# Strassen's seven products for pairs of up-projection tiles in a float32 two-layer trunk

## The chip, the cores and the metric

The kernel runs on one core of a Trainium2 chip. The metric is the time of one execution on the device in microseconds (us); three timed runs of the kernel before took 1123.32, 1124.51 and 1124.87.

## What is computed

512 tokens of 1024 features pass four sub-layers in float32: gated linear attention, an MLP, sliding-window attention, an MLP. Each is wrapped in norms, x <- x + RMSNorm_post(f(RMSNorm_pre(x))). The change concerns the MLPs, with D_FF = 4096:

```python
def sq_relu_mlp(h, w_up, w_down):
    return jnp.square(jax.nn.relu(h @ w_up)) @ w_down

for i in range(DEPTH):                      # DEPTH = 2
    h = rms_norm(x, ln_mix_pre[i])
    ...                                     # m: the token mixer of this layer
    x = x + rms_norm(m, ln_mix_post[i])
    h = rms_norm(x, ln_mlp_pre[i])
    f = sq_relu_mlp(h, mlp_w_up[i], mlp_w_down[i])
    x = x + rms_norm(f, ln_mlp_post[i])
```

## The kernel before

**Precision.** TensorE multiplies in a reduced float32 form. Every operand is split in two: h, a copy in that form by ScalarE (L83), and l, the rest, a subtraction by VectorE (L84, two inputs in SBUF). A product is three matmuls, h by h (L150), h by l (L151) and l by h (L152), `mm3`.

**Up projection.** `prenorm` scales each of four token tiles (128 tokens), transposes it on TensorE (L190) and splits it into four pairs of tiles hT, which hold features by tokens. The hidden features are made transposed: 32 tiles of 128 hidden features by 512 tokens, one accumulator each, eight k tiles of 128 features, three matmuls of 512 columns per k tile (`t_tile`, `t_step`). A tile's weights are one DMA of 512 KB into a `rawp` buffer (`weight`), split in halves of 512 columns. The first four tiles (NAHEAD) run earlier, in `t_ahead`: the matmuls of the first 256 tokens while the last token tiles of the sub-layer before are still being finished, then those of the other 256. ScalarE takes the Relu from PSUM (L702) and VectorE squares (L703).

**Down projection.** `natural` does two halves of 512 output features. For each of 32 k tiles `lhs` splits the hidden tile into two buffers (h, l) of the pool `tp` (17 buffers of 512 columns, `half`), and twelve matmuls follow: four token tiles by three. In the second half the last eight k tiles (TAIL) run token tile by token tile, and behind each one `evac`, `finish` and the next sub-layer's `prenorm` run: GpSimd computes the inverse roots in chains of five small operations (L124, L125, L127, L131, L132), ahead of which L182 or L216 prepares a term.

**Order.** Each engine executes its own queue in order. The order is set when the program is built, by a scheduler that follows priorities and dependencies; `later` and `tick` tie some instructions of the tail to matmuls. Buffers come from pools: `sp` (25 buffers of 1024 columns, `slot`), `tp` 17, `wp` 10 for split weights, `rawp` 3, and four PSUM pools of two banks (mm, ob, sc, tp). An instruction that writes into a buffer waits for the last reader of what was there. GpSimd has no work in the up stage.

Of the kernel before, what the change touches and what calls it, by code (L numbers as in the profile page):

```python
# [14 lines left out]
P = 128  # L15
# [13 lines left out]
ROWS = (slice(0, 64), slice(64, 128))  # L29
# The first steps in their order, each with its token tile or weight and half of the columns:  # L30
# P idle products, X load tokens, B spread the norm's gain, C load the identity, W load weights, q mean square,
# x gain, r root, s scale, t transpose, h and w split.
START = "P1 X0a P3 X0b X1 B0 C0 W0 W1 W2 q0 q1 x0a r0 s0a x0b X2 x1a t0a w0a x1b X3 s0b w1a s1a h0a t0b w0b t1a w2a w1b q2 W3 x2a s1b t1b h1a h0b x2b s2a h1b w2b t2a h2a w3a s2b q3 t2b w3b x3a h2b s3a x3b s3b t3a t3b h3a h3b"
# [5 lines left out]
def trunk(ctx: ExitStack, tc: tile.TileContext, x, vecs, g_qk, g_vg, g_lr, g_up, g_norm, g_out,  # L39
# [4 lines left out]
    const = ctx.enter_context(tc.tile_pool(name="const", bufs=1))  # L44
    rawp = ctx.enter_context(tc.tile_pool(name="rawp", bufs=3))
    wp = ctx.enter_context(tc.tile_pool(name="wp", bufs=10))
# [3 lines left out]
    tp = ctx.enter_context(tc.tile_pool(name="tp", bufs=17))  # L50
    st = ctx.enter_context(tc.tile_pool(name="st", bufs=64))
    ppool = {n: ctx.enter_context(tc.tile_pool(name="p" + n, bufs=b, space=bass.MemoryType.PSUM))
# [101 lines left out]
    def behind(insts, target):  # L154
        """Issue order only: the instructions come after the target on their engine."""
        for i in insts:
            tc.add_manual_dep(i.ins, target.ins.name, NOSYNC, reason="order")
# [3 lines left out]
    def later(when, insts):  # L161
        """Keeps instructions behind the matmul that ends this piece of a sub-layer's last part."""
        if ticks[0] is not None:
            plan.setdefault(when, []).extend(insts)
# [6 lines left out]
    def new_hT():  # L171
        return [(slot([P, 2, T], F32R, "hTh"), slot([P, 2, T], F32R, "hTl")) for _ in range(NK // 2)]

    def prenorm(t, wpre, hT):
# [10 lines left out]
        for q in range(2):  # L185
            part = slice(q * 512, (q + 1) * 512)
            later(4 * t + SCALE, [act.activation(xw[:, part], xw[:, part], AF.Copy, scale=r)])
            tb = tbank([P, 4, P])
            for k in range(4):
                later(4 * t + TURN, [pe.transpose(tb[:, k, :], xw[:, q * 512 + k * P:q * 512 + (k + 1) * P], ident)])  # L190
            for kk in range(2):
                h, l = hT[2 * q + kk]
                split(h[:, :, cols], l[:, :, cols], tb[:, 2 * kk:2 * kk + 2, :])
# [78 lines left out]

    def t_step(acc, w, hT, k, cols):
        (wh, wl), (h, l) = w, hT[k // 2]
        mm3(acc[:, cols], wh[:, k * P:(k + 1) * P], wl[:, k * P:(k + 1) * P],
            h[:, k % 2, cols], l[:, k % 2, cols], k == 0, k == NK - 1)

    def t_steps(src, hT, evac, n=None):
        """One T tile in pieces."""
        w = weight(src)  # L280
        acc = bank(n=n)
        for k in range(NK):
            t_step(acc, w, hT, k, slice(0, T))
            if k % 2 and k < NK - 1:
                yield
        evac(acc)
        yield

    def outer_steps(lhs, wd, acc):
        """The products for one half of the columns in pieces, all tokens at each k tile."""  # L290
        for kp in range(NK // 2):
# [39 lines left out]

# [1 line left out]
    def gla(hT, first, post, done):  # L333
# [229 lines left out]

# [1 line left out]
    def swa(hT, post, done):  # L565
# [35 lines left out]
        def queries():  # L601
            """The query heads' products in pieces."""
            for j in range(2, 8):
# [89 lines left out]

# [1 line left out]
    def mlp(layer, hT, post, done):  # L695
        a = []

        def ev(i, acc):
            if i % 2 == 0:
                a.append(slot([P, 2, T]))  # L700
            aa = a[-1][:, i % 2, :]
            act.activation(aa, acc, AF.Relu)  # L702
            dve.tensor_mul(aa, aa, aa)  # L703

        accs = t_ahead([m_up[layer, i] for i in range(NAHEAD)], hT)
        for i in range(NAHEAD):
            ev(i, accs[i])
        for i in range(NAHEAD, NF):
            ev(i, t_tile(m_up[layer, i], hT))

        def lhs(n, kp):
            r = []
            for i in range(2):
# [3 lines left out]
                else:  # L717
                    h, l = half([P, T], F32R), half([P, T], F32R)
                split(h, l, a[kp][:, i, :])
                r.append((h, l))  # L720
            return r
        natural(lhs, m_down[layer], NF, post.evac, TAIL, done)

# [1 line left out]
    warm = half([P, 512], F32R)  # L725
# [8 lines left out]
    def put(i):  # L734
        """Keeps the start's instructions on their engine in the order of START."""
        e = i.ins.engine
# [74 lines left out]
    for layer in range(2):  # L811
        nxt = new_hT()
        wpost, wpre = bcast(vecs[layer, 1]), bcast(vecs[layer, 2])
# [90 lines left out]
```

## Time and profile before

| | |
|---|---|
| timed runs, median | 1124.51 us (1123.32 to 1124.87) |
| profiled execution, span | 1120.4 us |
| TensorE (PE) busy | 1095.0 us, 98% |
| VectorE (DVE) busy | 592.0 us, 53% |
| ScalarE (ACT) busy | 523.3 us, 47% |
| GpSimd (POOL) busy | 107.7 us, 10% |
| moved by DMA | 108.11 MB, mean 96 GB/s |

The span is the time from the first to the last instruction of one profiled execution; the profile gives no other time for it, so the runs' median stands beside it. Busy is the time in which at least one instruction of the engine was under way; TensorE's weight loads have a row of their own (PEld) and overlap its matmuls. In the rows, "x<-a,b 128x512" is an operation with output x and inputs a and b, by the program's names. "[1.27 <-ACT xw L187]" behind a row is idle time ahead of it and what ended it. The first number of a timeline row is its start, the second its length; matmuls overlap, so their cost is read from start to start.

### The profile page before, as it was taken

To read this page: it belongs to the slowest core of one execution; us is meant where nothing else is said; L and a number is where in the kernel's file an instruction comes from. 1 tells how busy PE (TensorE), PEld (TensorE's weight loads), DVE (VectorE), ACT (ScalarE), POOL (GpSimd) and SP (SyncE) were. 2 spreads that over 40 slices of the span, in tenths; PEclk is the share of its full clock that TensorE was granted. 3 is DMA by queue.
4 is the path that set the end of the run, shared out by engine and by line. 5 is a ranking of instruction groups with operands and counts; after the bars stand their busy time and mean duration, and the time that the engine had idled before them with its cause. 6 is when DMAs were issued, how large, how long until landed. Compare 5 with 4: busy or idle time off the path is not lost.

```text
span 1120.4 us, 14561 instructions
## 1 busy us (share of the span) xinstructions
PE 1095.0 (98%) x5372; PEld 913.2 (82%) x5372; DVE 592.0 (53%) x1135; ACT 523.3 (47%) x1142; POOL 107.7 (10%) x283
## 2 busy tenths in 40 slices
PE   8999999999999999999999999999999999999997
PEld 5778887889888888888888899879888888888886
DVE  5676538476333334447427889667433334447423
ACT  6764435465323334446326688556432223446420
POOL 1021112250000000000015000043000000000002
PEclk9999999999999999999999999999999999999999
DMA  7412222223332223222223532104322232222212
GB/s 251 134 65 84 76 77 73 76 82 127 99 105 98 94 94 94 94 94 94 94 76 133 168 97 76 54 22 136 110 95 95 100 105 96 94 94 94 94 38 76
DMA packets 32153, 108.11 MB, mean 96 GB/s; under 512 B 3921, under 2 KB 4177, under 8 KB 32082
## 3 DMA queue, kind: packets, MB, share of 16 engines
q1 hardware_dynamic: 32082, 107.19, 29.4%
q8 instruction: 42, 0.69, 0.3%
q14 instruction: 29, 0.24, 0.1%
HBM read 100.88 MB, written 2.10 MB: 92 GB/s over the span
## 4 chain that ended last, share of the span: by engine, by line
PE 82%; POOL 5%; DVE 5%; ACT 3%; issue 2%; DMA 2%; SPq 0%; DVEq 0%; POOLq 0%; ACTq 0%
PE mm L150 15%; PE mm L152 15%; PE mm L151 15%; PE ob L151 5%; PE ob L152 5%; PE ob L150 5%; PE sc L152 3%; PE sc L151 3%; PE sc L150 3%; POOL st L125 2%; ACT junk L180 1%; POOL st L127 1%; PE sb L625 1%; POOL st L124 1%; PE pT L654 1%
## 5 line engine op out<-in xcount | busy, mean ns | idle before, releaser
L83 ACT CAST wh<-raw 128x512 fp32r<-128x512 f32 x348 | 206.5, 618 | 359.3 <-PE mm L151 236.7
L84 DVE TENSOR_TENSOR wl<-raw,wh 128x512 fp32r<-128x512 f32 x348 | 232.4, 691 | 253.3 <-ACT wh L83 253.1
L150 PE MATMUL mm<-hTh,wh 128*128 128x512 f32 x448 | 174.3, 389 | 0.0
L151 PE MATMUL mm<-hTl,wh 128*128 128x512 f32 x448 | 174.3, 389 | 0.0
L152 PE MATMUL mm<-hTh,wl 128*128 128x512 f32 x448 | 174.3, 389 | 0.0
L84 DVE TENSOR_TENSOR t<-s,t 128x512 fp32r<-128x512 f32 x112 | 77.5, 692 | 126.6 <-PE ob L151 66.8
L83 ACT CAST t<-s 128x512 fp32r<-128x512 f32 x112 | 69.4, 619 | 65.5 <-PE ob L152 42.8
L152 PEld LDWEIGHTS mm<-hTh,wl 128*128 128x128 f32 x448 | 84.1, 188 | 17.6
L151 PEld LDWEIGHTS mm<-hTl,wh 128*128 128x128 f32 x448 | 84.1, 188 | 17.4
L150 PEld LDWEIGHTS mm<-hTh,wh 128*128 128x128 f32 x448 | 84.1, 188 | 17.2
L151 PE MATMUL mm<-wl,t 128*128 128x512 f32 x224 | 88.3, 394 | 0.0
L150 PE MATMUL mm<-wh,t 128*128 128x512 f32 x224 | 88.2, 394 | 0.0
L152 PE MATMUL mm<-wh,t 128*128 128x512 f32 x224 | 88.2, 394 | 0.0
L216 POOL TENSOR_SCALAR st<-st 128x1 f32<-128x1 f32 x16 | 4.4, 277 | 554.0 <-ACT junk L212 520.7
L150 PEld LDWEIGHTS mm<-wh,t 128*128 128x128 f32 x224 | 42.0, 188 | 10.4 <-ACT s L702 0.5
L151 PE MATMUL ob<-wl,t 128*128 128x512 f32 x128 | 50.5, 394 | 0.0
L152 PE MATMUL ob<-wh,t 128*128 128x512 f32 x128 | 50.4, 393 | 0.0
L150 PE MATMUL ob<-wh,t 128*128 128x512 f32 x128 | 50.4, 393 | 0.0
L151 PEld LDWEIGHTS mm<-wl,t 128*128 128x128 f32 x224 | 42.1, 188 | 9.8
L152 PEld LDWEIGHTS mm<-wh,t 128*128 128x128 f32 x224 | 42.1, 188 | 9.7
L703 DVE TENSOR_TENSOR s<-s 128x512 f32<-128x512 f32 x64 | 43.8, 685 | 0.0
L151 PE MATMUL sc<-wl,t 128*128 128x512 f32 x96 | 37.9, 394 | 0.0
(292 smaller groups left out, 2249.9 us busy)
## 6 DMA issues: line engine op xcount, KB each, us to landing
raw<-in_m_up_dram SPq DMA_DIRECT2D x64, 512.0 KB, 3.4
raw<-in_m_down_dram SPq DMA_DIRECT2D x64, 512.0 KB, 3.4
raw<-in_g_vg_dram SPq DMA_DIRECT2D x16, 512.0 KB, 3.5
raw<-in_s_qkv_dram SPq DMA_DIRECT2D x10, 512.0 KB, 4.1
raw<-in_g_qk_dram SPq DMA_DIRECT2D x8, 512.0 KB, 4.4
raw<-in_g_out_dram SPq DMA_DIRECT2D x8, 512.0 KB, 3.6
q<-hl SPq DMA_DIRECT2D x32, 128.0 KB, 2.5
raw<-in_s_out_dram SPq DMA_DIRECT2D x8, 512.0 KB, 3.8
```

Of the source, the lines that this page charges most:

```text
L83: act.copy(h, src)
L84: dve.tensor_sub(l, src, f(h))
L124: pool.tensor_scalar(v, ss, scale, base, ALU.mult, ALU.add)
L125: pool.tensor_tensor(r0, v, mhalf[:, :n], ALU.pow)
L127: pool.tensor_scalar(t, v, r0, r0, ALU.mult, ALU.mult)
L150: pe.matmul(out_ap, lhsT=lh, rhs=rh, start=first, stop=False)
L151: pe.matmul(out_ap, lhsT=lh, rhs=rl, start=False, stop=False)
L152: newest[0] = pe.matmul(out_ap, lhsT=ll, rhs=rh, start=False, stop=last)
L180: act.activation(junk, xt[:, part], AF.Square, accum_out=ss[:, i:i + 1])
L625: newest[0] = pe.matmul(sb[:, e, :], lhsT=q[:, e, pc], rhs=k2[:, i, win], start=i == 0, stop=i == 1)
L654: pe.transpose(tb[:, e, jj, :], p[:, e, c:c + P], ident)
L703: dve.tensor_mul(aa, aa, aa)
```

## The change

For each MLP the 32 up tiles are seen as two rows of 16 (tile i and tile i+16), the 1024 input features as two halves (512 each, q = 0, 1), the tokens as two halves of 256. So a pair of tiles is a 2x2 block product: 2 blocks of hidden features, 2 of tokens, summed over 2 of input features. Four tiles, (0, 16, 1, 17), still run ahead as before (both token halves in one accumulator). The other 28 make 14 pairs. A pair is computed by Strassen's scheme in Winograd's form with seven block products M1 to M7, each of four k tiles by three matmuls of 256 columns.

The sums that the scheme needs of the tokens (S1 to S4) are formed once per MLP in `Blocks.put`, as each token tile has been transposed: f = h + l for the first two token tiles on GpSimd, S3 and S1 on VectorE, a copy on ScalarE, S2 and S4 on GpSimd; `sums` splits them. The sums of the weights are formed for each pair in `prepare`: four subtractions of 128x512 on GpSimd, then four splits (three of 1024 columns: lo, tt, hi; one of 512: b21). The products go into three accumulators A, B and C of 256 columns, in the order M1, M2, M6, M7, M5, M4, M3, with M6, M5 and M3 added to what stands in A; copies and adds take the four blocks of the result out (a0, a1), and Relu and square are one VectorE operation per tile. Two pairs are in flight, half a pair apart. The first seven pairs of hidden tiles stand in `tp` buffers, two each, and the others in `sp`. The rows of the down weights are reordered on the host to the pairs' order. `rawp` has 4 buffers in place of 3, `st` 48 in place of 64.

```diff
-    rawp = ctx.enter_context(tc.tile_pool(name="rawp", bufs=3))
+    rawp = ctx.enter_context(tc.tile_pool(name="rawp", bufs=4))
...
-    st = ctx.enter_context(tc.tile_pool(name="st", bufs=64))
+    st = ctx.enter_context(tc.tile_pool(name="st", bufs=48))
...
+    class Blocks:
+        def __init__(self):
+            self.hl, self.f, self.s = {}, {}, {}
+        def put(self, t, q, tb):
+            th, p = divmod(t, 2)
+            cols = slice(p * P, (p + 1) * P)
+            if p == 0:
+                self.hl[th, q] = slot([P, 4, 256], F32R, "bh"), slot([P, 4, 256], F32R, "bl")
+                if th == 0:
+                    self.f[q] = slot([P, 4, 256], n="bf")
+            h, l = self.hl[th, q]
+            split(h[:, :, cols], l[:, :, cols], tb)
+            if th == 0:
+                pool.tensor_add(self.f[q][:, :, cols], f(h)[:, :, cols], f(l)[:, :, cols])
+            elif q == 0:
+                self.tb = tb
+            else:
+                if p == 0:
+                    self.s = {i: slot([P, 4, 256], n=f"S{i}") for i in (1, 2, 3, 4)}
+                s1, s2, s3, s4 = (self.s[i][:, :, cols] for i in (1, 2, 3, 4))
+                dve.tensor_sub(s3, self.f[0][:, :, cols], self.tb)
+                act.copy(s2, self.tb)
+                dve.tensor_add(s1, s2, tb)
+                pool.tensor_sub(s2, s1, self.f[0][:, :, cols])
+                pool.tensor_sub(s4, self.f[1][:, :, cols], s2)
+        def sums(self):
+            r = {1: self.hl[0, 0], 2: self.hl[0, 1], 4: self.hl[1, 1]}
+            for m, i in ((7, 3), (5, 1), (6, 2), (3, 4)):
+                h, l = slot([P, 4, 256], F32R, "Sh"), slot([P, 4, 256], F32R, "Sl")
+                split(h, l, self.s[i])
+                r[m] = h, l
+            return r
...
+            if isinstance(hT, Blocks):
+                hT.put(t, q, tb)
+                continue
...
     def t_step(acc, w, hT, k, cols):
+        if isinstance(hT, Blocks):
+            (wh, wl), (h, l) = w, hT.hl[cols.start // 256, k // 4]
+            mm3(acc[:, cols], wh[:, k * P:(k + 1) * P], wl[:, k * P:(k + 1) * P], h[:, k % 4], l[:, k % 4], k == 0, k == NK - 1)
+            return
...
-        a = []
-
-        def ev(i, acc):
-            if i % 2 == 0:
-                a.append(slot([P, 2, T]))
-            aa = a[-1][:, i % 2, :]
+        a = {}
+        def hidden(i):
+            if i < 7:
+                a[i] = half([P, T], n=f"a{i}"), half([P, T], n=f"a{i}")
+            else:
+                both = slot([P, 2, T], n=f"a{i}")
+                a[i] = both[:, 0], both[:, 1]
+            return a[i]
+        fs = [i + NF // 2 * j for i in range(NAHEAD // 2) for j in range(2)]
+        accs = t_ahead([m_up[layer, i] for i in fs], hT)
+        for i, acc in enumerate(accs):
+            aa = hidden(i // 2)[i % 2] if i % 2 == 0 else a[i // 2][1]
             act.activation(aa, acc, AF.Relu)
             dve.tensor_mul(aa, aa, aa)
 
-        accs = t_ahead([m_up[layer, i] for i in range(NAHEAD)], hT)
-        for i in range(NAHEAD):
-            ev(i, accs[i])
-        for i in range(NAHEAD, NF):
-            ev(i, t_tile(m_up[layer, i], hT))
+        S = hT.sums()
+        def prepare(i):
+            lo, hi = (rawp.tile([P, 2, 512], F32, tag="raw", name=name("raw")) for _ in range(2))
+            nc.sync.dma_start(lo, m_up[layer, i].rearrange("p (a b) -> p a b", a=2))
+            nc.sync.dma_start(hi, m_up[layer, i + NF // 2].rearrange("p (a b) -> p a b", a=2))
+            b11, b21, b12, b22 = lo[:, 0], lo[:, 1], hi[:, 0], hi[:, 1]
+            tt = slot([P, 2, 512], n=f"tt{i}")
+            def parts(src):
+                n = src.shape[1] if len(src.shape) == 3 else 1
+                h, l = (wp.tile([P, n, 512], F32R, tag="w", name=name("w")) for _ in range(2))
+                split(h, l, src if n > 1 else src.rearrange("p (a b) -> p a b", a=1))
+                return [(h[:, k], l[:, k]) for k in range(n)]
+            w = {}
+            w[1], w[2] = parts(lo)
+            pool.tensor_sub(tt[:, 1], b22, b12)
+            pool.tensor_sub(b12, b12, b11)
+            pool.tensor_sub(tt[:, 0], b22, b12)
+            w[6], w[7] = parts(tt)
+            w[5], w[3] = parts(hi)
+            pool.tensor_sub(b21, b21, tt[:, 0])
+            w[4], = parts(b21)
+            return w
+        def pair(i):
+            w = prepare(i)
+            yield
+            A, B, C = bank((P, 256), ("mm", "tp")[i // 2 % 2], f"A{i}"), bank((P, 256), "ob", f"B{i}"), bank((P, 256), "sc", f"C{i}")
+            lo, hi = slice(0, 256), slice(256, 512)
+            for m, acc in ((1, A), (2, B), (6, A), (7, C), (5, A), (4, C), (3, A)):
+                (wh, wl), (h, l) = w[m], S[m]
+                for k in range(4):
+                    kc = slice(k * P, (k + 1) * P)
+                    fresh = m in (1, 2, 7)
+                    first, last = fresh and k == 0, k == 3
+                    pe.matmul(acc, lhsT=wh[:, kc], rhs=h[:, k], start=first, stop=False, skip_group_check=not fresh)
+                    pe.matmul(acc, lhsT=wh[:, kc], rhs=l[:, k], start=False, stop=False, skip_group_check=not fresh)
+                    pe.matmul(acc, lhsT=wl[:, kc], rhs=h[:, k], start=False, stop=last, skip_group_check=not fresh)
+                if m == 1:
+                    a0, a1 = hidden(i)
+                    act.copy(a0[:, lo], A)
+                elif m == 2:
+                    dve.tensor_add(a0[:, lo], a0[:, lo], B)
+                elif m == 6:
+                    act.copy(a0[:, hi], A)
+                elif m == 7:
+                    pass
+                elif m == 5:
+                    act.copy(a1[:, hi], A)
+                    dve.tensor_add(a1[:, hi], a1[:, hi], C)
+                elif m == 4:
+                    dve.tensor_add(a0[:, hi], a0[:, hi], C)
+                elif m == 3:
+                    act.copy(a1[:, lo], A)
+                    for x in (a0, a1):
+                        dve.scalar_tensor_tensor(out=x, in0=x, scalar=0.0, in1=x, op0=ALU.max, op1=ALU.mult)
+                yield
+        live, order = [], [pair(i) for i in range(NAHEAD // 2, NF // 2)]
+        for g in order[:2]:
+            next(g)
+        nxt, steps = 2, 0
+        live = [order[0]]
+        pend = [order[1]]
+        while live or pend:
+            for g in list(live):
+                if next(g, 0) == 0:
+                    live.remove(g)
+                    if pend:
+                        live.append(pend.pop(0))
+                        next(live[-1], 0)
+                        if nxt < len(order):
+                            next(order[nxt])
+                            pend.append(order[nxt])
+                            nxt += 1
+            steps += 1
+            if steps == 4 and pend:
+                live.append(pend.pop(0))
+                if nxt < len(order):
+                    next(order[nxt])
+                    pend.append(order[nxt])
+                    nxt += 1
 
         def lhs(n, kp):
             r = []
@@ -716,12 +852,12 @@
                     h, l = hl[:, 0, :], hl[:, 1, :]
                 else:
                     h, l = half([P, T], F32R), half([P, T], F32R)
-                split(h, l, a[kp][:, i, :])
+                split(h, l, a[kp][i])
                 r.append((h, l))
             return r
...
-        nxt = new_hT()
+        nxt = Blocks()
...
+    pairs = np.arange(FF).reshape(2, NF // 2, P).transpose(1, 0, 2).reshape(FF)
...
-        "m_down": np.stack([nlay(w) for w in a["mlp_w_down"]]),
+        "m_down": np.stack([nlay(w[pairs]) for w in a["mlp_w_down"]]),
```

The order of VectorE's queue in the middle of the up projection, before: splits of weights (wl from raw and wh) and squares (s):

```order
L84 TENSOR_TENSOR wl_606_3524<-raw_604_3521,wh_605_3523 128x512
L84 TENSOR_TENSOR wl_610_3559<-raw_608_3556,wh_609_3558 128x512
L703 TENSOR_TENSOR s_584_3375<-s_584_3375 128x512
L84 TENSOR_TENSOR wl_610_3559<-raw_608_3556,wh_609_3558 128x512
L84 TENSOR_TENSOR wl_615_3595<-raw_613_3592,wh_614_3594 128x512
L703 TENSOR_TENSOR s_593_3446<-s_593_3446 128x512
```

The same place now, where pairs 10, 11 and 12 meet (w from raw or tt are splits, a the hidden tiles, B and C accumulators in PSUM):

```order
L84 TENSOR_TENSOR w_654_3640<-raw_647_3624,w_653_3639 128x1024
L812 TENSOR_TENSOR a10_645_3621<-a10_645_3621,C10_644_3608 128x256
L814 TENSOR_TENSOR a10_645_3621<-a10_645_3621,C10_644_3608 128x256
L805 TENSOR_TENSOR a11_660_3755<-a11_660_3755,B11_658_3741 128x256
L84 TENSOR_TENSOR w_656_3645<-raw_646_3623,w_655_3644 128x512
L818 SCALAR_TENSOR_TENSOR a10_645_3621<-a10_645_3621 128x512
L84 TENSOR_TENSOR w_665_3763<-raw_661_3757,w_664_3762 128x1024
L84 TENSOR_TENSOR w_667_3770<-tt12_663_3761,w_666_3769 128x1024
L818 SCALAR_TENSOR_TENSOR a10_645_3621<-a10_645_3621 128x512
L84 TENSOR_TENSOR w_669_3774<-raw_662_3758,w_668_3773 128x1024
L812 TENSOR_TENSOR a11_660_3755<-a11_660_3755,C11_659_3742 128x256
```

The add of C (L812) stands behind the splits of lo, tt and hi of the next pair and a square. On GpSimd's queue, where the last two tokens' roots of the first mixer are computed, before:

```order
L125 TENSOR_TENSOR st_431_2206<-st_430_2205,mhalf_100 128x1
L127 TENSOR_SCALAR st_432_2207<-st_430_2205,st_431_2206 128x1
L131 TENSOR_SCALAR st_432_2207<-st_432_2207 128x1
L132 TENSOR_TENSOR st_433_2208<-st_432_2207,st_431_2206 128x1
L124 TENSOR_SCALAR st_436_2260<-st_389_2039,st_390_2042 128x1
L125 TENSOR_TENSOR st_437_2261<-st_436_2260,mhalf_100 128x1
L127 TENSOR_SCALAR st_438_2262<-st_436_2260,st_437_2261 128x1
```

and now, with L190 of the changed kernel being the sum of h and l of a transposed tile:

```order
L125 TENSOR_TENSOR st_442_2274<-st_441_2273,mhalf_100 128x1
L190 TENSOR_TENSOR bf_416_2140<-bh_414_2138,bl_415_2139 128x4x128
L127 TENSOR_SCALAR st_443_2275<-st_441_2273,st_442_2274 128x1
L131 TENSOR_SCALAR st_443_2275<-st_443_2275 128x1
L132 TENSOR_TENSOR st_444_2276<-st_443_2275,st_442_2274 128x1
L124 TENSOR_SCALAR st_455_2337<-st_384_2037,st_385_2040 128x1
L190 TENSOR_TENSOR bf_420_2152<-bh_418_2150,bl_419_2151 128x4x128
L125 TENSOR_TENSOR st_456_2338<-st_455_2337,mhalf_100 128x1
L127 TENSOR_SCALAR st_457_2339<-st_455_2337,st_456_2338 128x1
```

Two sums of 128x512 stand inside the two chains. Last, TensorE's queue in the first half of the down projection, where a new k tile begins (the first three rows of twelve before, of which the next three repeat the pattern; t are the halves of the hidden tile), before:

```order
L150 MATMUL mm_616_3626<-wh_656_3832,t_658_3838 128x512 [waits Activation_49]
L151 MATMUL mm_616_3626<-wl_657_3833,t_658_3838 128x512 [waits DVE_49]
L152 MATMUL mm_616_3626<-wh_656_3832,t_659_3839 128x512 [waits DVE_49]
L150 MATMUL mm_617_3627<-wh_656_3832,t_658_3838 128x512
L151 MATMUL mm_617_3627<-wl_657_3833,t_658_3838 128x512
L152 MATMUL mm_617_3627<-wh_656_3832,t_659_3839 128x512
```

and now, with the last two matmuls of the k tile before ahead of it:

```order
L151 MATMUL ob_724_4370<-wl_734_4414,t_737_4423 128x512
L152 MATMUL ob_724_4370<-wh_733_4413,t_738_4424 128x512
L150 MATMUL mm_721_4367<-wh_740_4453,t_742_4459 128x512 [waits Activation_49]
L151 MATMUL mm_721_4367<-wl_741_4454,t_742_4459 128x512
L150 MATMUL mm_722_4368<-wh_740_4453,t_742_4459 128x512
L152 MATMUL mm_721_4367<-wh_740_4453,t_743_4460 128x512 [waits DVE_49]
L151 MATMUL mm_722_4368<-wl_741_4454,t_742_4459 128x512
```

The matmul that reads l (t_743) has moved behind one of the next token tile, and it is the one that waits for VectorE. l of a k tile takes the buffer that h of the k tile before (t_737) held.

## Rows read from the trace of the kernel before

**Rows 1.** Busy time, share and instructions of each engine; the ended-last chain by engine.
```profile
PE 1095.0 (98%) x5372; PEld 913.2 (82%) x5372; DVE 592.0 (53%) x1135; ACT 523.3 (47%) x1142; POOL 107.7 (10%) x283
...
PE 82%; POOL 5%; DVE 5%; ACT 3%; issue 2%; DMA 2%; SPq 0%; DVEq 0%; POOLq 0%; ACTq 0%
```

**Rows 2.** Windows, up and down: span, five engines' busy, clock, DMA share, GB/s.
```profile
320.00:340.00 20.00, 20.00 (x90) 16.57 (x89) 7.58 (x12) 6.50 (x12) 0.00 (x0) 1.00 0.24 84
460.00:480.00 20.00, 20.00 (x88) 16.20 (x87) 9.10 (x15) 8.14 (x15) 0.00 (x0) 1.00 0.31 105
```

**Rows 3.** Timeline of TensorE: up stage, ahead stage, down stage; start, length, instruction.
```profile
361.59 0.39 PE L150 MATMUL mm<-hTh,wh 128*128 128x512 f32 x1
365.67 0.39 PE L150 MATMUL mm<-hTh,wh 128*128 128x512 f32 x1
255.97 0.28 PE L150 MATMUL ob<-hTh,wh 128*128 128x256 f32 x1
261.97 0.28 PE L152 MATMUL sc<-hTh,wl 128*128 128x256 f32 x1
459.88 0.39 PE L150 MATMUL mm<-wh,t 128*128 128x512 f32 x1
465.43 0.39 PE L150 MATMUL mm<-wh,t 128*128 128x512 f32 x1
```

**Rows 4.** Timeline of the down stage: a matmul and the splits behind it.
```profile
462.19 0.39 PE L151 MATMUL ob<-wl,t 128*128 128x512 f32 x1
462.67 1.14 ACT L83 CAST wh<-raw 128x512 fp32r<-128x512 f32 x2 [1.97 <-PE ob L151]
462.68 0.69 DVE L84 TENSOR_TENSOR t<-s,t 128x512 fp32r<-128x512 f32 x1 [2.08 <-PE ob L151]
463.32 1.29 DVE L84 TENSOR_TENSOR wl<-raw,wh 128x512 fp32r<-128x512 f32 x2
```

**Rows 5.** Instructions grouped by line and shape: busy us, mean ns, idle before, releaser.
```profile
L84 DVE TENSOR_TENSOR wl<-raw,wh 128x512 fp32r<-128x512 f32 x348 | 232.4, 691 | 253.3 <-ACT wh L83 253.1
L83 ACT CAST wh<-raw 128x512 fp32r<-128x512 f32 x348 | 206.5, 618 | 359.3 <-PE mm L151 236.7 <-PE ob L151 79.3 <-issue 22.9
L84 DVE TENSOR_TENSOR hTl<-tp,hTh 128x256 fp32r<-128x256 f32 x48 | 19.0, 418 | 9.3 <-ACT hTh L83 8.9
L483 ACT COPY sn<-dS 128x256 f32<-128x256 f32 x4 | 1.5, 371 | 2.2 <-PE dS L152 2.2
```

**Rows 6.** Timeline of VectorE and GpSimd in the first mixer, and GpSimd alone later.
```profile
79.48 0.68 DVE L414 SCALAR_TENSOR_TENSOR r<-g,r 128x512 f32<-128x512 f32 x1
79.69 1.61 POOL L419 TENSOR_TENSOR gt<-g,gn 128x512 f32<-128x512 f32 x1 [1.89 <-PE Tk L151]
80.09 1.77 DVE L84 TENSOR_TENSOR wl<-raw,wh 128x512 fp32r<-128x512 f32 x1
82.53 1.65 POOL L419 TENSOR_TENSOR gt<-g,gn 128x512 f32<-128x512 f32 x1 [1.23 <-DVE g L415]
82.98 0.68 DVE L444 TENSOR_TENSOR kf<-Tk,E 128x512 f32<-128x512 f32 x1
184.76 1.30 POOL L419 TENSOR_TENSOR gt<-g,gn 128x512 f32<-128x512 f32 x1 [1.62 <-DVE g L415]
```

**Rows 7.** Timeline: first and last of ten root operations in a row, and the transposes.
```profile
239.73 0.51 POOL L124 TENSOR_SCALAR st<-st,st 128x1 f32<-128x1 f32 x1 [0.84 <-ACT junk L180]
244.84 0.19 POOL L132 TENSOR_TENSOR st<-st,st 128x1 f32<-128x1 f32 x1
252.33 0.66 PE L190 MATMUL tp<-cst,xw 128*128 128x128 f32 x4 [1.27 <-ACT xw L187]
```

**Rows 8.** Timeline of a mixer's output projection: a late split and TensorE behind it.
```profile
716.02 0.69 DVE L84 TENSOR_TENSOR ol<-ob,oh 128x512 fp32r<-128x512 f32 x1 [1.68 <-ACT oh L83]
716.76 0.19 PEld L150 LDWEIGHTS ob<-wh,oh 128*128 128x128 f32 x1 [0.21 <-DVE ol L84]
717.10 0.39 PE L151 MATMUL ob<-wl,oh 128*128 128x512 f32 x1
```

## Prediction

> **What bounds the kernel now.** I read the busy shares first, then the chain that ended last, then the up and down stages in windows, and only then single rows. TensorE is busy 98% of the span and the chain runs through it for 82% [rows 1]. In 20 us of the up projection it is busy all 20.00 at granted clock 1.00, while VectorE works 7.58, ScalarE 6.50, GpSimd 0.00 and the DMA engines 0.24; the down projection has 20.00 of TensorE too, with 9.10 and 8.14 beside it [rows 2]. So in both stages the end is set by how many columns TensorE streams, and the other engines have more than half their time free. A change that takes columns away gains just as long as the other engines stay ahead with the work it puts on them.
>
> The profiled span is 1120.4 us; the median of the runs is 1124.51, so 4.1 us lie outside the span. I carry all differences over to the median.
>
> **TensorE's saving.** In the up stage 18 matmuls of 512 columns start between 361.59 and 365.67, so one takes 0.2267 us. In the part that runs ahead in halves, 50 matmuls of 256 columns start between 255.97 and 261.97, each after its own weight load: 0.120 us [rows 3]. Two tiles were 2 x 8 x 3 = 48 wide matmuls, 48 x 0.2267 = 10.88 us. A pair is now 7 products x 4 k tiles x 3 = 84 narrow ones, 84 x 0.120 = 10.08 us. One eighth of the columns goes, but the narrow matmul costs 6% more per column, so only 0.80 us of 10.88 is left. 14 pairs in each of two MLPs: 28 x 0.80 = **-22.4 us**.
>
> **What the pairs put on the other engines.** Prices: a VectorE split or product of 128x512 is 691 ns (0.60 from start to start in a row of two), 1024 columns about 1.22 us, 256 columns with one input in PSUM 0.42; a ScalarE copy of 512 is 618 ns, of 1024 about 1.05, of 256 from PSUM 371 ns [rows 4, 5]. A GpSimd operation of 128x512 ran 1.30 us when nothing was beside it, some 1.15 of it after a start of 0.15 [rows 6]. VectorE per pair: three splits of 1024 (3.66), one of 512 (0.60), two squares (1.20), three adds from PSUM (1.26), 6.7 us. ScalarE: 3 x 1.05 + 0.62 + 4 x 0.37 = 5.3. GpSimd: four subtractions, 5.2. Each fits alone under 10.08.
>
> They don't stand alone. At 79.48 a VectorE operation with two inputs in SBUF is running; GpSimd's product starts at 79.69 and ends 1.14 after VectorE's end at 80.16; the VectorE split of 80.09, some 0.7 us by itself, takes 1.77, that is until 0.56 after GpSimd's end. The one at 82.98 that reads PSUM takes 0.68 with GpSimd's 82.53 beside it [rows 6]. So an operation of GpSimd and one of VectorE with both inputs in SBUF exclude each other, for their whole length, in turn. Per pair that is 4 x 1.15 + 3.66 + 0.60 + 1.20 = 10.1 us of a resource held by one at a time, against 10.08 of TensorE.
>
> [...]
>
> The place where it hurts is the first matmul of M4 of each pair: it may only start once VectorE has added C into the hidden tile (L812), and in VectorE's queue that add stands behind lo split, tt split, a square and the hi split. Without exclusion the chain from the lo split's start to the end of L812 is 3 x 1.22 + 0.60 + 0.42 = 4.7 us. With it the tt split, the square and the hi split each let one subtraction of GpSimd go first, because b21's subtraction and the next pair's first three lie exactly there: 3 x 1.15 = 3.45 more, 8.1 us. I walked three stretches of two pairs through the queue rows with these prices and found TensorE waiting 1.83, 3.2 and 1.54 us, mean 2.2, so 1.1 a pair. Without exclusion the same walk gives 0.24 a pair; if all of VectorE's and GpSimd's work were one queue, 6.7 + 5.2 - 10.1 = 1.8. I take 1.09 a pair for the 26 pairs that have one before them: **+28.4 us** (6 to 47).
>
> **Start of the pairs.** Before the first pair, GpSimd has S2 and S4 of two token tiles (4 operations) and then seven subtractions that stand ahead of the b21 split, behind which ScalarE's copy of M1's result is queued; M6 of the second pair waits for that copy. 11 x 1.30 = 14.3, plus about 3.5 for VectorE's part before and the splits and copy behind, and up to three holds by VectorE, 3.5: 17.8 to 21.3 us after the last transposes. TensorE has for that time four tiles' second halves (96 x 0.120 = 11.5) and M1 and M2 (24 x 0.120 = 2.9), 14.4. The difference is 3.4 to 6.9; I take the upper end, 7, since the steady walk found most holds taken: **+14** for the two MLPs (1 to 10 each; the small end is 11 x 1.15 with three of the other steps beside it, the large one has every GpSimd operation at 1.6).
>
> **The end of the sub-layer before.** The last two tokens' root chains run back to back on GpSimd from 239.73 to 245.03, and the transposes behind them start late, after 1.27 us of idle TensorE [rows 7]. The change puts four 128x512 sums there; two stand inside the chains of the last tokens (the order rows show them), 2 x 1.3 to 1.65. I take 3 us per MLP: **+6** (1.3 to 5 each; the small end if one of them falls in an idle gap).
>
> **The down projection.** Seven hidden tiles now occupy 14 of the 17 buffers from which the down projection's two halves h and l come, so 3 are left, and the l of a k tile can be made only when the h of the tile before was read for the last time, by the 11th of its 12 matmuls. VectorE's split starts 0.49 after that matmul's start (462.19, 462.68) and takes 0.69. Where a weight load waits for such a split, it starts 0.05 behind it (716.71, 716.76), and the matmul after the waiting one starts at 717.10, 0.39 behind it [rows 4, 8]. The reader of l is now the 4th matmul of the next k tile, five on from the 11th; the one after it starts 0.49 + 0.69 + 0.39 = 1.57 after the 11th, and by the pitch (24 starts from 459.88 to 465.43, 0.2312 [rows 3]) it would be six on, 1.39. 0.18 us x 31 k tiles x 2 MLPs = **+11.2** (8 to 18, as VectorE is late by another split or not). In the other column half the buffers are free again: nothing. The last pair, alone at the end of the up stage, waits some 0.7: **+1.4**. Nothing else moves: the weights' bytes are the same, and the DMA share of 0.24 leaves room.
>
> Sum: -22.4 + 28.4 + 14 + 6 + 11.2 + 1.4 = **+38.6**, 1124.5 + 38.6 = **1163 us**.
>
> **Rivals.**
> First, exclusion costs nothing: the chain to L812 stays at 4.7 us plus one hold, TensorE's other pair covers it. For it: GpSimd's wait is cheap when VectorE happens to be in a PSUM operation. Then -22.4 + 0 + 2 + 3 + 11.2 + 1.4 = -4.8, 1120 us, faster. It decides at the point where the chain from lo split to L812 is under some 6 us. Against it: the 1.77 and 1.61 us rows [rows 6].
> Second, one queue: VectorE and GpSimd never overlap and set the pace, +47 + 20 + 10 + 18 + 1.4 - 22.4 = +74, 1198 us. For it: 10.1 of 10.08 us are held already.
> Third, the change doesn't save what it says: narrow matmuls with a weight load each would fall to the load's 0.19 [rows 8], 84 x 0.19 = 16.0 instead of 10.88, 28 x 5.1 = +143. Against it: the 50 starts in 6.00 us, each with its load.
> Fourth, the l split is early enough (ScalarE and VectorE queues order it otherwise): 11.2 less, 1152 us.
>
> **Chances.** Forecast 0.60 with the fourth beside it 0.05, one queue 0.18, exclusion free 0.15, narrow matmuls slow 0.02. About 2.2 us (0.2%) can be told from no change. The first rival, and the low tail of the forecast where it runs into it (0.03), give 1120 to 1127: of these 0.18, faster 0.14 and same 0.04; all else is slower, 0.82. The range takes in the low sum of all small ends (-22.4 + 6 + 2 + 2.6 + 8 + 1.4 = -2.4, 1122) and the second rival: 1122 to 1198.
>
> **What would show it.** Up stage: 84 narrow matmuls per pair at 0.120 us (else the third rival), TensorE idle of about 1 us a pair ended by VectorE's L812, and VectorE splits of 1024 at 2.3 instead of 1.2 us with GpSimd's subtractions at 1.3 to 2.4 beside them. If the splits are 1.2, the first rival. Start: some 7 us of TensorE idle in M6, ended by ScalarE. Down, first half: 0.18 us of weight-load idle per k tile, ended by VectorE's split. The forecast is wrong if TensorE stays above 97% busy through the up stage.

## The result and the profile after

The changed kernel took 1168.59 us (median of four runs, 1162.64 to 1168.75) against 1123.91 (1122.47 to 1124.87): 1.039 times the time, 95% interval 1.0366 to 1.0416. It is slower, by 44.7 us where 38.6 were forecast. The profiled spans are 1167.0 and 1120.4 us, 46.6 apart, and the account below is made against those.

From the profile's page of the changed kernel, busy times, the granted clock by slices and the chain by engine:

```profile
PE 1103.2 (95%) x6380; PEld 955.5 (82%) x6380; DVE 762.7 (65%) x1219; ACT 582.8 (50%) x1194; POOL 330.7 (28%) x411
...
PEclk9999999988999999999999999988899999999999
...
PE 72%; DVE 12%; POOL 7%; ACT 5%; issue 4%; DMA 1%; SPq 0%; DVEq 0%; POOLq 0%; ACTq 0%
```

Against [rows 1], GpSimd has three times the busy time, VectorE 171 us more, and the chain of the end has moved from TensorE (82%) to VectorE and GpSimd (12% and 7% in place of 5% each). TensorE's busy time should have fallen by 22 us; it rose by 8, in part because TensorE ran at a lower clock at the start of each MLP (the slices of 8: two, then three), and in part because the stall in the down projection's first halves shows as busy time (90.63 us busy of 90.63). What TensorE waited for, in the changed kernel (total us, times, longest):

```profile
PE C L798 <- DVE a L812: 17.9, 15, 1.8
PE A L798 <- ACT a L803: 12.1, 2, 6.5
PE tp L228 <- ACT xw L225: 9.8, 8, 2.1
PE ob L150 <- ACT bh L83: 4.7, 2, 2.5
```

and the same view of the kernel before, where these two were the rows of the tails:

```profile
PE tp L190 <- ACT xw L187: 3.6, 4, 1.3
PE ob L150 <- ACT hTh L83: 2.4, 3, 1.5
```

By stretches, from the starts of TensorE's matmuls in both traces (us more than before, first MLP and second):

| stretch | forecast, both | measured | both |
|---|---|---|---|
| tail: first transposes to the end of the tiles ahead | +6 | +7.5, +7.9 | +15.4 |
| up: first pair to the end of the down projection's first k tile | +21.4 | +11.6, +11.6 | +23.2 |
| down, first column half | +11.2 | +4.3, +4.7 | +9.0 |
| down, second half (first MLP) | 0 | 0.0 | 0 |

The rows add up to 47.6 us. What lies ahead of the first MLP took 1.5 us less in this execution, and the rest of the span 0.5 more.

In the up projection, where TensorE never idled [rows 2], it waits for L812 once or so in two pairs. One such wait, in the timeline of the three engines:

```profile
327.27 1.22 DVE L84 TENSOR_TENSOR w<-raw,w 128x1024 fp32r<-128x1024 f32 x1
329.23 1.78 DVE L84 TENSOR_TENSOR w<-tt,w 128x1024 fp32r<-128x1024 f32 x1 [0.74 <-ACT w L83]
330.94 1.78 DVE L818 SCALAR_TENSOR_TENSOR a<-a 128x512 f32<-128x512 f32 x1
332.64 2.31 DVE L84 TENSOR_TENSOR w<-raw,w 128x1024 fp32r<-128x1024 f32 x1
334.87 0.41 DVE L812 TENSOR_TENSOR a<-a,C 128x256 f32<-128x256 f32 x1
...
328.63 1.30 POOL L783 TENSOR_TENSOR raw<-raw,tt 128x512 f32<-128x512 f32 x1 [2.88 <-DVE w L84]
329.91 2.25 POOL L778 TENSOR_TENSOR tt<-raw 128x512 f32<-128x512 f32 x1
332.24 1.62 POOL L779 TENSOR_TENSOR raw<-raw,raw 128x512 f32<-128x512 f32 x1
333.94 2.14 POOL L780 TENSOR_TENSOR tt<-raw 128x512 f32<-128x512 f32 x1
...
335.33 0.39 PE L798 MATMUL C<-bh,w 128*128 128x256 f32 x1 [1.75 <-DVE a L812]
```

As in [rows 6], the square of 0.7 us takes 1.78 and the hi split of 1.22 takes 2.31, each stretched by an operation of GpSimd, and GpSimd's by VectorE's; the add that reads PSUM takes its 0.41 with GpSimd beside it. From the lo split to the end of L812 it is 8.0 us; 8.1 were worked out. The parts agree less well: 0.74 of the 8.0 is a wait for ScalarE's copy that the prediction's chain did not have, and GpSimd lengthened the three operations by 2.7 us in place of 3.45. Behind this wait comes something that was not worked out. The windows on that place (span; busy of TensorE, weight loads, VectorE, ScalarE, GpSimd; granted clock; DMA share; GB/s):

```profile
330.00:336.00 6.00, 4.25 (x35) 4.04 (x35) 6.00 (x5) 2.37 (x5) 5.84 (x3) 1.00 0.01 3
336.00:340.00 4.00, 4.00 (x23) 4.00 (x22) 2.96 (x6) 1.63 (x2) 0.08 (x1) 0.57 0.45 132
340.00:344.00 4.00, 4.00 (x36) 4.00 (x35) 3.13 (x3) 2.07 (x4) 2.45 (x2) 1.00 0.39 131
```

One microsecond after TensorE has started again, the clock is granted at its lower level (1.2 GHz, 0.5 in this column) for some 3.5 us, and 16 matmuls start 0.21 us apart instead of 0.12: 16 x 0.09 = 1.5 us more, nearly as much as the wait itself. In the two tails and up projections there are ten such stretches, six of 3.4 us and four of 6.8, all in or behind waits of 1.75 us and more; the kernel before had one there, behind a wait of 1.54 us. Counted from start to start against the pace at full clock, they cost 18.1 us in all, against 1.5 before.

### The profile page after: what moved, and what is told of

Same layout as the page of the kernel before. It is cut to its first block, busy times and chain, and to the rows that moved or that the text cites. A ratio compares the mean times of both kernels' runs of the same rounds, so it can differ in the third digit from the quotient of the medians.

```text
span 1167.0 us, 16975 instructions
## 1 busy us (share of the span) xinstructions
PE 1103.2 (95%) x6380; PEld 955.5 (82%) x6380; DVE 762.7 (65%) x1219; ACT 582.8 (50%) x1194; POOL 330.7 (28%) x411
## 4 chain that ended last, share of the span: by engine, by line
PE 72%; DVE 12%; POOL 7%; ACT 5%; issue 4%; DMA 1%; SPq 0%; DVEq 0%; POOLq 0%; ACTq 0%
PE mm L152 7%; PE mm L150 7%; PE mm L151 7%; PE ob L152 5%; PE ob L151 5%; PE ob L150 5%; DVE w L84 4%; PE A L798 4%; PE A L799 4%; PE A L800 3%; PE sc L152 3%; PE sc L150 3%; PE sc L151 3%; PE C L798 2%; PE C L799 2%
## 5 line engine op out<-in xcount | busy, mean ns | idle before, releaser
L83 ACT CAST wh<-raw 128x512 fp32r<-128x512 f32 x236 | 139.7, 619 | 151.6 <-PE ob L151 79.5
L84 DVE TENSOR_TENSOR wl<-raw,wh 128x512 fp32r<-128x512 f32 x236 | 159.0, 697 | 68.2 <-ACT wh L83 66.1
L84 DVE TENSOR_TENSOR t<-a,t 128x512 fp32r<-128x512 f32 x112 | 78.8, 704 | 110.0 <-PE ob L151 82.7
L84 DVE TENSOR_TENSOR w<-raw,w 128x1024 fp32r<-128x1024 f32 (+1 forms) x84 | 113.9, 1356 | 15.4 <-ACT w L83 15.4
L83 ACT CAST w<-raw 128x1024 fp32r<-128x1024 f32 (+1 forms) x84 | 75.4, 906 | 89.8 <-PE C L799 72.8
L798 PE MATMUL A<-Sh,w 128*128 128x256 f32 x336 | 98.5, 293 | 12.1 <-ACT a L803 12.1
L83 ACT CAST t<-a 128x512 fp32r<-128x512 f32 x112 | 68.7, 619 | 64.2 <-PE ob L152 47.2
L799 PE MATMUL A<-Sl,w 128*128 128x256 f32 x336 | 97.9, 291 | 0.0
L800 PE MATMUL A<-Sh,w 128*128 128x256 f32 x336 | 97.7, 291 | 0.0
L798 PEld LDWEIGHTS A<-Sh,w 128*128 128x128 f32 x336 | 67.8, 202 | 12.9 <-ACT a L803 12.5
L799 PEld LDWEIGHTS A<-Sl,w 128*128 128x128 f32 x336 | 67.6, 201 | 0.0
L800 PEld LDWEIGHTS A<-Sh,w 128*128 128x128 f32 x336 | 67.4, 201 | 0.0
```

Source lines behind the costliest of these rows:

```text
L83: act.copy(h, src)
L84: dve.tensor_sub(l, src, f(h))
L798: pe.matmul(acc, lhsT=wh[:, kc], rhs=h[:, k], start=first, stop=False, skip_group_check=not fresh)
L799: pe.matmul(acc, lhsT=wh[:, kc], rhs=l[:, k], start=False, stop=False, skip_group_check=not fresh)
L800: pe.matmul(acc, lhsT=wl[:, kc], rhs=h[:, k], start=False, stop=last, skip_group_check=not fresh)
```

## The experiments

Times are medians; "before" ran beside each (1123.0).

**GpSimd's sums in the tail**

```diff
-                pool.tensor_add(self.f[q][:, :, cols], f(h)[:, :, cols], f(l)[:, :, cols])
+                act.copy(self.f[q][:, :, cols], tb)
```

> The sum f of the first two token tiles is made by ScalarE as a copy of the transposed tile from PSUM (the same value) in place of GpSimd's h + l. Theory A: the two sums that stand inside the root chains of GpSimd make the two tails late; in the changed kernel the stretches from the tails' first transposes to the end of the four tiles that run ahead are 7.5 and 7.9 us longer than before, idle time and the slow clock after it together. Without the sums they come back to 1 to 3 us each: 10 to 14 us less in all, about 1156 us. Rival B: the tails are late because a tile is split only when all four blocks are transposed and because S3, copy and S1 follow one another; then the time falls by at most 4 us.

Measured 1156.02 us (1.029, 1.0266 to 1.0315), as theory A had it. The tails are 2.9 and 1.9 us longer than before in place of 7.5 and 7.9. In the changed kernel's trace one sees why a sum between the steps of a root costs so much, in the first tail and then in the second:

```profile
242.12 1.29 POOL L190 TENSOR_TENSOR bf<-bh,bl 128x512 f32<-128x512 f32 x1
243.39 1.82 POOL L127 TENSOR_SCALAR st<-st,st 128x1 f32<-128x1 f32 x1
...
772.25 1.81 POOL L127 TENSOR_SCALAR st<-st,st 128x1 f32<-128x1 f32 x1
775.75 0.66 PE L228 MATMUL tp<-cst,xw 128*128 128x128 f32 x4 [2.08 <-ACT xw L225]
```

The sum takes its 1.29, and the one-column step of the root behind it takes 1.82 where it took 0.34 elsewhere in the same chains (ten steps of these chains took 5.3 us together before [rows 7]), while five splits of VectorE stand beside it. In the second tail the transposes behind such a step come late: TensorE idles 2.08 us, and a microsecond after 775.75 its granted clock is at the lower level. In e1 the wait of the transposes is 5.7 us in place of 9.8, and that for ScalarE's copy bh 2.0 in place of 4.7.

**The weights' subtractions on VectorE** (four lines like this)

```diff
-            pool.tensor_sub(b12, b12, b11)
+            dve.tensor_sub(b12, b12, b11)
```

> The four weight subtractions of a pair run on VectorE in place of GpSimd. Theory A (GpSimd and VectorE exclude each other): VectorE gets 4 x 0.60 us more work per pair, 9.1 of 10.1 us, but its splits of 1024 columns take 1.2 in place of up to 2.3 us; the wait for L812 falls from 17.9 us to under 8, the wait at the start of the pairs from 12.1 to under 4, the slow clock in the pairs' stage goes: 20 to 35 us less, 1134 to 1149 us. Rival B (the add L812 is late because of its place in VectorE's queue, and the queue gets longer): the wait for L812 stays at 15 us or grows, only the start gains: 0 to 10 us less.

Measured 1130.89 us (1.0065, 1.0043 to 1.0087), 37.7 less than the changed kernel, a little more than theory A's 20 to 35. The wait for L812 is 0.8 us in all, that at the start of the pairs is 1.7, and the up stretches are 6.9 and 7.3 us shorter than before:

```profile
PE A L798 <- ACT a L803: 1.7, 2, 1.2
PE C L798 <- DVE a L812: 0.8, 2, 0.5
```

Groups of VectorE (busy us, mean ns), first of the changed kernel, then of this one:

```profile
L84 DVE TENSOR_TENSOR w<-raw,w 128x1024 fp32r<-128x1024 f32 x56 | 86.6, 1546 | 13.9 <-ACT w L83 13.9
L818 DVE SCALAR_TENSOR_TENSOR a<-a 128x512 f32<-128x512 f32 x56 | 62.6, 1117 | 0.5
```

```profile
L84 DVE TENSOR_TENSOR w<-raw,w 128x1024 fp32r<-128x1024 f32 x56 | 68.3, 1220 | 0.8 <-ACT w L83 0.8
L818 DVE SCALAR_TENSOR_TENSOR a<-a 128x512 f32<-128x512 f32 x56 | 38.3, 687 | 0.7
L779 DVE TENSOR_TENSOR raw<-raw,raw 128x512 f32<-128x512 f32 x28 | 19.3, 690 | 0.6
```

VectorE now does 112 operations more (four groups of 28 at 0.69 us, 77 us), and its busy time is 762.2 us where it was 762.7. The busy time it had before was, to that amount, waiting.

**More buffers for the down projection**

```diff
-                if n == 1 and kp >= (NF - TAIL) // 2:
+                if n == 0 and kp > 0 or n == 1 and kp >= (NF - TAIL) // 2:
```

> From the second pair of k tiles on, the first half of the down projection puts its h and l into buffers of the pool sp that are free by then, so none of them waits for the k tile before. Theory A: the two first halves, 4.3 us longer each than before, come back: 8.7 us less, about 1160 us, and the split l starts well ahead of its reader. Rival B: the stall has another cause (VectorE's queue, the weights' splits): no change over 2 us.

Measured 1154.85 us (1.028, 1.0253 to 1.0306), 13.7 less. The first column half is 6.1 and 6.3 us shorter, and so 1.7 us shorter than in the kernel before; the second up stretch was 5 us shorter as well, and that is not the edit's doing: none of the five waits of 1.75 us for L812 there had the half clock behind it, where two of three had in the changed kernel, and the half clock cost 1.4 us in place of 5.8. That the stall was the buffers is shown. One k tile's begin in the changed kernel, where the third matmul shown is the first that reads l and waits for it, and the next start comes 0.34 later in place of 0.23:

```profile
520.58 0.39 PE L151 MATMUL mm<-wl,t 128*128 128x512 f32 x1
520.81 0.40 PE L150 MATMUL mm<-wh,t 128*128 128x512 f32 x1
521.05 0.50 PE L152 MATMUL mm<-wh,t 128*128 128x512 f32 x1
521.39 0.40 PE L151 MATMUL mm<-wl,t 128*128 128x512 f32 x1
```

**Work for TensorE in its longest wait**

```diff
+                if m == 2 and i == NAHEAD // 2:
+                    for _ in range(48):
+                        pe.matmul(C, lhsT=w[1][0][:, :P], rhs=S[1][0][:, 0], start=True, stop=True)
```

> 48 matmuls of 256 columns that nobody reads stand between M2 and M6 of the first pair of each MLP, where TensorE waits 6.7 and 5.7 us. They end before the wait does, or nearly. Theory A: the clock is granted at half after TensorE's idle, and the 20 or so matmuls that follow at 0.229 us cost about 2 us per MLP; with the dummies they run at 0.12: 2 to 5 us less in all. Rival B: the slow clock does not come from the idle time: no change, 0.229 stays, or up to 2 us more where the dummies end late.

Measured 1162.49 us (1.036, 1.0319 to 1.04), 6 less for 96 matmuls more; the interval overlaps the changed kernel's and one run of four was at 1169.8, so the time alone does not settle it. The traces are clear. The changed kernel, and then this one:

```profile
281.26 0.58 PE L798 MATMUL A<-Sh,w 128*128 128x256 f32 x1 [6.55 <-ACT a L803]
281.64 0.41 PE L799 MATMUL A<-Sl,w 128*128 128x256 f32 x1
```

```profile
275.39 5.92 PE L803 MATMUL C<-bh,w 128*128 128x256 f32 x48
281.15 0.28 PE L798 MATMUL A<-Sh,w 128*128 128x256 f32 x1
281.27 0.28 PE L799 MATMUL A<-Sl,w 128*128 128x256 f32 x1
```

M6 begins at nearly the same moment, but at 0.12 us per matmul where it was 0.21. The 24 matmuls of M6 and M7 take 2.9 us from start to start where they took 4.7, and in the second MLP 3.0 where they took 5.3. So the half clock comes from the idle time, and costs 1.8 and 2.3 us at this place. The up stretches as a whole are 3.2 and 2.5 us shorter, other waits having moved as well.

**Does GpSimd's work harm where nobody waits for it?** As e2, and in addition

```diff
+            for x in (b22, b22, b11, b11):
+                pool.tensor_sub(junk, x, cst[:, :512])
```

> As e2 (subtractions on VectorE), but GpSimd does four subtractions of 128x512 per pair as well, each of a weight block and a constant, into a tile that nobody reads in this stage. Nothing waits for them but the reuse of the weights' buffer. Theory A (exclusion alone makes the loss): VectorE's splits of 1024 columns go from 1.22 back to 1.5 or more, and with 9.1 us of VectorE and 4.6 of GpSimd to be held in turn per 10.1 us the pairs' stage gets at least 8 us longer per MLP than in e2: 1147 to 1185 us. Rival B (the loss came from waiting for GpSimd's results, 1.3 us each against 0.6): within 4 us of e2, 1127 to 1135.

Measured 1263.12 us (1.1253), outside both ranges. It is no clean test: GpSimd's operations read the weights, and GpSimd idled 200.9 us for their DMA. By the trace the issue of that DMA waited for VectorE's late splits (307.9 us in 24 waits), while the next expectation takes GpSimd's own reads for the cause, which no row shows. So a second test, as e2 with the operations on data whose buffers nothing needs:

```diff
                         dve.scalar_tensor_tensor(out=x, in0=x, scalar=0.0, in1=x, op0=ALU.max, op1=ALU.mult)
+                    for _ in range(4):
+                        pool.tensor_sub(junk, a0, a1)
```

> As e2 (subtractions on VectorE), and GpSimd does four subtractions of 128x512 after each pair, a0 - a1 of its finished hidden tiles, into a tile that nobody reads in this stage. In e6 they read the weights' buffers and kept them from the next DMA; here no buffer and no engine waits for them. Theory A (exclusion): VectorE's splits of 1024 columns take 1.5 us or more on the mean in place of 1.22; VectorE's 9.1 and GpSimd's 4.6 us have to go in turn, some 12.5 us without the operations that read PSUM, against 10.1 of TensorE: 28 x 2.4 = 67 us and the slow clock on top, 1190 to 1230 us, and at the least 1145. Rival B (the loss of the changed kernel and of e6 came from waiting for GpSimd's results and from the buffers it held): within 4 us of e2, 1127 to 1135.

Measured 1231.86 us (1.0968, 1.095 to 1.0985), just above theory A's range: 101 us more than e2 for operations that nobody waits for. TensorE's wait for L812, VectorE's groups and, in the timeline, one pair of neighbours:

```profile
PE C L798 <- DVE a L812: 56.9, 24, 4.9
L84 DVE TENSOR_TENSOR w<-raw,w 128x1024 fp32r<-128x1024 f32 x56 | 83.3, 1487 | 0.0
L779 DVE TENSOR_TENSOR raw<-raw,raw 128x512 f32<-128x512 f32 x28 | 38.8, 1387 | 0.6
```

```profile
345.52 0.69 DVE L778 TENSOR_TENSOR tt<-raw 128x512 f32<-128x512 f32 x1
345.75 7.22 POOL L820 TENSOR_TENSOR junk<-a,a 128x512 f32<-128x512 f32 x4 [5.77 <-DVE a L818]
346.24 1.68 DVE L779 TENSOR_TENSOR raw<-raw,raw 128x512 f32<-128x512 f32 x1
```

So the exclusion alone makes such a loss, whatever is computed: the wait for L812 goes from 0.8 to 56.9 us, and some 32 us of half clock, counted from start to start, come with the waits. How the changed kernel's 37.7 us divide between exclusion and waiting for GpSimd's results is not shown. The Trainium skill (SBUF — State Buffer, Who interferes with whom) says that a VectorE instruction with two SBUF inputs contends with a GpSimd instruction that reads SBUF. It calls the ports that the two share an exclusive lock. This run agrees: VectorE's subtraction of 0.69 us takes 1.68 beside GpSimd's four, and these take 7.22 us where one alone took 1.30 [rows 6].

**All three edits**, with S2 and S4 on VectorE:

> All three edits at once: f as ScalarE's copy, the four weight subtractions on VectorE, the down projection's first half in buffers of sp; S2 and S4 are formed on VectorE as well, so GpSimd has only the roots. If the terms add up as each showed alone (per MLP: tail 5, pairs 18.7, down 6.2 us less than in the changed kernel), 60 us less than 1168.6: about 1108 us, 1.4% under the kernel before, and of the change's 22.4 us most is there. Rival: they don't add up, since VectorE is now busy 9.1 of 10.1 us and has the S sums as well, so the start of the pairs gets late: 1115 to 1125 us.

Measured 1109.41 us (0.9873, 0.9852 to 0.9895), where 1108 was worked out: the terms add up, though the move of S2 and S4 was not run alone. Stretches against before: tails +3.1 and +2.6, up -7.3 and -7.6, down -1.8 and -1.6.

```profile
PE 1078.3 (97%) x6380; PEld 948.1 (85%) x6380; DVE 753.7 (68%) x1339; ACT 584.5 (53%) x1202; POOL 104.4 (9%) x283
```

**One of the four subtractions back on GpSimd** (that of b21)

> As e5_all, with one of the four subtractions of a pair (b21, the one needed last) back on GpSimd. If what counts is the sum that must go in turn, it is now 3.66 + 0.60 + 1.20 + 1.80 of VectorE and 1.15 of GpSimd, 8.4 of 10.1 us: theory A expects the time of e5_all within 4 us, 1105 to 1114. Rival B: any operation of GpSimd in the chain from the lo split to L812 delays it by its whole length, so 26 times up to 1.15 us: 1120 to 1140.

Measured 1120.72 us (0.9982, 0.9971 to 0.9993), 11 more than e5: outside theory A's range and at the low end of rival B's. L812 is waited for again, but briefly:

```profile
PE C L798 <- DVE a L812: 7.4, 15, 0.7
```

So the sum that must go in turn (8.4 of 10.1 us) doesn't decide alone: one block in a queue that must be on time costs about 0.4 us a pair, less than its whole length.

**The matmul's 0.231 and 0.227 us.** The kernel before with e3's edit, e5 with all of the second half in sp as well, and the kernel before with the pool tp declared first:

> The kernel before, with the down projection's h and l of the first half in buffers of sp from the second pair of k tiles on. In e3 that half ended up 1.7 us per MLP shorter than in the kernel before, at 0.227 us per matmul where the kernel before has 0.231. Theory A: matmuls whose stationary operand lies in the buffers of tp are that much slower, whatever the rest does: 3.4 us less, 0.3%. Rival B: the 1.7 us came from the changed kernel's other order: no change over 1 us.

> As e5_all, with the second half of the down projection in sp too. If the matmul is faster from there (0.227 in place of 0.231), 24 k tiles x 12 x 0.0045 = 1.3 us per MLP less than e5_all, about 1105 us. Rival: the buffers of sp run short while the next sub-layer's norm starts, a tail waits, and the time is that of e5_all or more.

> The kernel before, with the pool tp declared first, so that it lies at other addresses; nothing else is changed. Theory A: the 0.231 in place of 0.227 us per matmul of the down projection comes from where the stationary operand lies: the pitch changes, and with it up to 6 us. Rival B: it comes from one operand being in two buffers (h and l apart) in place of one: the pitch stays at 0.231 and the time within 1 us.

e7: 1120.58 us (0.9979, 0.9966 to 0.9991), the first halves 1.9 and 1.8 us shorter, the other stretches of the MLPs within 0.15: a gain of 0.2% at the edge of what can be told, but plain in the trace, where 12 starts take 2.71 us, 0.226 each, against 0.231 in [rows 3]:

```profile
464.74 0.39 PE L152 MATMUL mm<-wh,s 128*128 128x512 f32 x1
467.45 0.39 PE L152 MATMUL mm<-wh,s 128*128 128x512 f32 x1
```

e8: 1112.92 us (0.9908, 0.9889 to 0.9927). The second half was 1.4 us shorter as worked out, but the first lost 2.5 where the two halves meet, in a wait for ScalarE's split (4.6 us in two); by the median it is 3.5 us behind e5, though its profiled span is 1.5 us shorter (1108.6 and 1110.1), so whether it is slower isn't settled; the gain of theory A did not come. e10: 1123.83 us (1.0009, 0.9998 to 1.0019), each stretch within 0.05 us of before: this other address changes nothing. Whether it is one buffer in place of two or something else in sp stays open.

## Why the prediction was right, and where it was off

The time (1163 against 1168.6) and the mechanism were right; the sizes of its steps were less even than the sum, and one cost, the half clock behind TensorE's waits, stood in none of them.

- **TensorE's saving, -22.4.** Right: the narrow matmuls run at 0.120 us wherever TensorE has its full clock, and e5 shows 7.3 and 7.6 of the 11.2 us per MLP, the rest being short waits.
- **Steady waits, +28.4, and the end of the up stage, +1.4.** Right in sum, and wrong in what it is made of. With the start's 17.1 taken off, the up stretches leave 23.2 + 22.4 - 17.1 = 28.5. Counted from start to start, 20.0 of that are the waits for L812 (17.9 of idle time, 1.4 us in two pairs where the walk had 2.2), 6.0 the half clock behind four of them, and 2.5 small delays. That this sum came out is in part luck: the waits were put some 8 us too high, and the half clock at nothing.
- **Start of the pairs, +14.** The wait was 6.7 and 5.7 us from start to start, close to the 7 that were forecast; the half clock behind it, 4.6 us in both MLPs, makes it 17.1. e2 takes GpSimd's queue away and with it all but 1.7 us of the wait.
- **The tail, +6.** The step that was mis-sized: 15.4. I charged each sum its own 1.3 to 1.65 us; but the step of the root that stands behind it was stretched too, and the clock fell twice per tail: counted from start to start, longer waits make some 10 of the 15.4 and the half clock 6. e1 gives 10.6 of it back in the trace; the rest is the wider split and the S sums, not separated.
- **Down, +11.2.** The cause was right (e3), the size 9.0: 0.14 us per k tile in place of 0.18.
- **First rival** (exclusion free): it needed the chain to L812 under 6 us; it was 8.0. **One queue**: 1198 was not reached, and the add on PSUM above ran its 0.41 us beside GpSimd's operation. **Slow narrow matmuls**: no. **Early l**: no.
- The mark "TensorE idle about 1 us a pair" held at 0.7, the mark "0.18 of weight-load idle" at 0.14 by the length of the stretch. VectorE's splits of 1024 columns took 1.55 us on the mean, with 2.31 beside GpSimd in the row above. TensorE was busy for 91% of the first up stretch (151.21 of 166.80 us), under the 97% that would have spoken against the forecast.

## What to carry to other kernels

Before moving elementwise work to an idle GpSimd, look whether VectorE's operations in that stage read two operands from SBUF: if they do, GpSimd's time comes out of VectorE's, and 4 x 0.6 us on VectorE was cheaper here than 4 x 1.3 us beside it, by 38 us. Where TensorE bounds a stage, its waits may be paid for twice: four of the six waits of 1.75 us for L812 had matmuls at half the clock behind them, and half-clock stretches make 18.1 us of this kernel's tails and up projections. When three costs have three causes, undo each alone: worked out by stretches, the gains added up to within 2 us, and together they turned 4% slower into 1.3% faster.

## What the runs showed of the hardware that was not expected

- TensorE's granted clock fell behind some idle times of 1.75 us and not behind others: after the waits that ended at 335.33 and 403.20 it did, after the one at 381.04, as long, it did not. The four waits of 1.20 us for L812 had no such stretch behind them, but one wait of 1.54 us in the kernel before (ended at 755.22) had. The windows behind 381.04 and behind 403.20 (clock: 1.00 and 0.59):

```profile
384.00:388.00 4.00, 4.00 (x36) 4.00 (x35) 3.97 (x5) 2.35 (x5) 1.96 (x1) 1.00 0.37 131
404.00:408.00 4.00, 4.00 (x24) 4.00 (x23) 2.79 (x5) 1.59 (x2) 0.00 (x0) 0.59 0.43 148
```

- VectorE's busy time in a profile contains its waits for GpSimd: 762.7 us with them, and 762.2 in e2, where GpSimd has no weight subtractions and VectorE 77 us more work.
- A one-column operation of GpSimd is stretched by VectorE as a wide one is: 1.82 us in place of 0.34.
- With the stationary operand in a buffer of sp, the down projection's matmuls start every 0.226 to 0.227 us in place of 0.231; the cause is open.
